# Second FFN's up-projection: the moving operand read from its two halves in turn, with halves and weights at several byte distances

## The chip, the cores and the metric

One core of one Trainium2 chip. The metric is the device time of one execution in microseconds (us), as the median of the runs shown. The engines are TensorE (PE in the profile, with its weight loads as PEld), VectorE (DVE), ScalarE (ACT), GpSimd (POOL) and SyncE (SP), which issues the DMAs.

## The reference, cut to what matters

Two layers over 512 latent tokens and 256 context tokens of 1024 features: layer 0 attention, layer 1 a bidirectional Mamba-2 mixer, each followed by a gated FFN. The change touches the FFN of layer 1, which has the latent tokens alone (512):

```python
def conv_ffn(h, w_up, conv_w, conv_b, w_down):
    g, u = jnp.split(h @ w_up, 2, axis=-1)          # h (512, 1024), w_up (1024, 2 * 2816)
    g = dwconv_centred(g, conv_w, conv_b)           # width 3, along the tokens
    return (jax.nn.silu(g) * u) @ w_down
...
h_l = modulate(rms_norm(x, norm_ffn_w[i]), mod_l[3], mod_l[4])
x = x + mod_l[5] * conv_ffn(h_l, ffn_w_up[i], ffn_conv_w[i], ffn_conv_b[i], ffn_w_down[i])
```

## The kernel before

All activations lie with features on the 128 partitions and tokens along the free dimension, so that 1024 features are KT = 8 tiles of 128x512. Every product is made of three matmuls in fp32r (`mm3`, L100 to L108): a number is split into a high and a low part, and the results of high weight by high activation (L105), high weight by low activation (L106) and low weight by high activation (L108) are summed in PSUM. `split` (L78) makes the parts: ScalarE casts the high part (L85), VectorE subtracts to get the low part (L87). `load_w` (L90) loads a 128x1024 weight tile by DMA on SP's queue into `wst` and splits it into `wh` and `wl`. All three come from one pool tag `t4` with 10 buffers of 4096 bytes.

The second FFN is `ffn(g, 1, ...)`, called at the end of `body`. Its up-projection has 44 weight tiles: f = 0 to 21 for the gate, 22 + f for the other branch. For each f, `up(f)` computes the gate tile (`gemm(f)`, 8 k-steps of three matmuls of 128x512), ScalarE reads it out of PSUM with the middle tap of the convolution (`cv`, L834), VectorE adds the two outer taps, reading the same PSUM tile twice (L838, L839), ScalarE applies SiLU (L840), the second tile `gemm(22 + f)` is computed, VectorE multiplies (`hd`, L849), and the product is split into `hdh` and `hdl`. The hidden tiles of two f are kept; after the first up of the next pair, `down` multiplies them by their two rows of w_down (8 output tiles `ps_d`) and adds the result to x (L785).

PSUM: pool tag S has 2 buffers of two banks each, used for `ps_first` and `ps_up`; pool tag B (`Bank`) has 4 buffers of one bank. The first two up tiles (f = 0 and 22) are not computed in `ffn` but in `first_tiles`, while the norm ahead still produces the modulated activations `h`: in two halves of 256 tokens, with `hhf` (high) written by ScalarE and `hlf` (low) by VectorE or GpSimd. Their two results lie in the two S buffers until `up(0)` has read them. For f = 1 and 23, `gemm` takes a B buffer for that reason (`ps_up1`); all later ones take S.

Within an engine the instructions stand in the order that a scheduler chose from the program's order, the dependences and the buffers; each engine works off its own list in that order and waits on semaphores. SBUF tiles of the second FFN other than weights come from a pool `pg` that is opened after the mixer's pools are closed, with tag `t3` (24 buffers).

Of the kernel before, what the change touches and what calls it, by code (L numbers as in the profile page):

```python
# [7 lines left out]
P = 128  # L8
F32 = mybir.dt.float32
F32R = mybir.dt.float32r  # L10
# [6 lines left out]
KT = D // P  # L17
L = 512
# [49 lines left out]
def t3(g, name, dt=F32, n=T):  # L68
    return g.t3p.tile([P, n], dt, tag="t3", bufs=g.n3, name=name)


def t4(g, name, dt=F32):
    return g.p.tile([P, 1024], dt, tag="t4", bufs=10, name=name)
# [7 lines left out]
def split(g, src, hi, lo, lo_engine="dve", pin=False):  # L81

    nc = g.nc
    keep = g.tc.keep_in_program_order if pin else lambda i: i
    keep(nc.scalar.copy(hi, src))  # L85
    eng = nc.vector if lo_engine == "dve" else nc.gpsimd
    keep(eng.tensor_tensor(lo, src, _r(hi), ALU.subtract))  # L87


def load_w(g, dram, lo_engine="dve", pin=False):  # L90

    st = t4(g, "wst")
    wh = t4(g, "wh", F32R)
    wl = t4(g, "wl", F32R)
    g.nc.sync.dma_start(st, dram)
    split(g, st, wh, wl, lo_engine=lo_engine, pin=pin)
    return wh, wl


def mm3(g, w, outs, first, last):  # L100

    wh, wl = w
    mm = g.nc.tensor.matmul
    for out, (ah, al) in outs:
        mm(out, wh, ah, start=first, stop=False)  # L105
        mm(out, wh, al, start=False, stop=False)  # L106
    for out, (ah, al) in outs:
        mm(out, wl, ah, start=False, stop=last)  # L108
# [106 lines left out]
def follow(g, bi):  # L215

    if g.last_act is not None:
        g.tc.add_manual_dep(bi.ins, g.last_act.ins.name, mybir.DependencyInfo(
            mybir.DependencyClass.NoSync, mybir.DependencyReason.DATA), reason="order of tables")
    g.last_act = bi  # L220


def ln_exp(g):
    follow(g, g.nc.scalar.preload_act_table_set("natural_log_exp_and_others"))
# [77 lines left out]
def S(g, name):  # L302
    return g.ps.tile([P, 1024], F32, tag="S", bufs=2, name=name)


def Bank(g, name):
    return g.ps.tile([P, 512], F32, tag="B", bufs=4, name=name)
# [44 lines left out]
def gemm_in(g, tiles, h, off, segs):  # L352


    for run in segs:
        for ps, w in tiles:
            for k in range(KT):
                ks = slice(k * P, (k + 1) * P)
                mm3(g, (w[0][:, ks], w[1][:, ks]),
                    [(ps[:, off[i] + a : off[i] + b], tuple(t[:, a:b] for t in h[i][k])) for i, a, b in run],  # L360
                    k == 0, k == KT - 1)
                yield


def firsts(g, *units):
    return [load_w(g, u) for u in units]
# [430 lines left out]
def ffn(g, layer, streams, x, h, first, nxt=None, side=iter(()), after=()):  # L797

    nc, I = g.nc, g.I
    ns = len(streams)
    tot = sum(n for n, _ in streams)
    off = [0, L]

    cw = [g.par[:, PC[f"fw{layer}{t}"] : PC[f"fw{layer}{t}"] + NFT] for t in range(3)]
    cb = g.par[:, PC[f"fb{layer}"] : PC[f"fb{layer}"] + NFT]
    whole = [[(i, 0, n) for i, (n, _) in enumerate(streams)]]

    def gemm(t):  # L810

        if t % NFT == 0:
            ps = first[t // NFT]
        else:
            w = load_w(g, I["wup"][layer, t])
            if t % NFT == 1:
                out = []
                for i in range(ns):
                    ps = Bank(g, "ps_up1")
                    for _ in gemm_in(g, [(ps, w)], h, (0, 0), [[s] for s in whole[0] if s[0] == i]):  # L820
                        pass
                    out.append((ps, [i]))
                return [(ps[:, : streams[i][0]], off[i], off[i] + streams[i][0], i) for ps, (i,) in out]
            ps = S(g, "ps_up")
            for _ in gemm_in(g, [(ps, w)], h, off, [[s] for s in whole[0]]):
                pass
        return [(ps[:, :tot], 0, tot, None)]

    def up(f):
        pg = gemm(f)  # L830
        cv = t3(g, "cv", n=tot)
        w0, w1, w2 = (c[:, f : f + 1] for c in cw)
        for ps, a, b, _ in pg:
            nc.scalar.activation(cv[:, a:b], ps, AF.Identity, scale=w1, bias=cb[:, f : f + 1])  # L834
        for i in range(ns):
            a, b = off[i], off[i] + streams[i][0]
            ps, o = next((ps, o) for ps, o, e, j in pg if j in (None, i))
            nc.vector.scalar_tensor_tensor(cv[:, a + 1 : b], ps[:, a - o : b - o - 1], w0, cv[:, a + 1 : b], ALU.mult, ALU.add)  # L838
            nc.vector.scalar_tensor_tensor(cv[:, a : b - 1], ps[:, a - o + 1 : b - o], w2, cv[:, a : b - 1], ALU.mult, ALU.add)  # L839
        follow(g, nc.scalar.activation(cv, cv, AF.Silu))  # L840
        some = (2, 2, 2, 3)[f] if ns > 1 and f < 4 else 1
        for _ in range(some):
            next(side, None)
        pu = gemm(NFT + f)
        for _ in range(some):
            next(side, None)
        hd = t3(g, "hd", n=tot)
        for ps, a, b, _ in pu:
            nc.vector.tensor_tensor(hd[:, a:b], cv[:, a:b], ps, ALU.mult)  # L849
        hi, lo = t3(g, "hdh", F32R, n=tot), t3(g, "hdl", F32R, n=tot)  # L850
        split(g, hd, hi, lo)
        return [(hi[:, off[i] : off[i] + streams[i][0]], lo[:, off[i] : off[i] + streams[i][0]]) for i in range(ns)]

    gate = g.mod[layer][5]
    segs, f = [], 0
    for n in [3] + [2] * 8 + [3] if nxt else [2] * 11:
        segs.append(range(f, f + n))
        f += n
    acts, pend, wf = {}, None, []

    def flush(fs, order, norm=None, after=None):
        ws = [load_w(g, I["wdown"][layer, f * P : (f + 1) * P]) for f in fs]
        if after:
            wf.extend(firsts(g, *after))
        return down(g, ws, [acts.pop(f) for f in fs], gate, streams, x, order, norm, side=side)

    for fs in segs:
        for j, f in enumerate(fs):
            acts[f] = up(f)
            if j == 0 and pend:  # L870
                flush(pend, whole)
        pend = fs
    for _ in side:
        pass
    if nxt:
        ln_exp(g)
    return flush(pend, [[s] for s in ending(streams)], nxt, after), wf
# [378 lines left out]
def body(nc, tc, I, out, dbg=None):  # L1256
    g = Ctx()
# [3 lines left out]
    pool = lambda n, st=es, **k: st.enter_context(tc.tile_pool(name=n, bufs=1, **k))  # L1261
# [31 lines left out]
    x = [[X[:, m, a:b] for m in range(KT)] for a, b in ((0, L), (L, T))]  # L1293
# [23 lines left out]
    phf = ExitStack()  # L1317
# [19 lines left out]

    x, nrm, first = ssd(g, x, nxt, wf, bg, close)
    phf = ExitStack()
    g.t3p, g.n3 = pool("pg", phf), 24  # L1340
    if not (dbg and dbg.get("stage") == 3):
        ffn(g, 1, [(L, 0)], x, nrm.h, first)
    for m in range(KT):
# [103 lines left out]
```

## Time and profile before

| what | value |
|---|---|
| median of the runs (1914.01 and 1917.44) | 1915.72 us |
| span of the profiled execution, first to last instruction | 1908.8 us |
| its time outside the span | not listed; the median is 6.9 us above the span |
| TensorE busy | 1875.1 us (98%) |
| VectorE, ScalarE, GpSimd busy | 1312.3, 820.3, 307.3 us |
| DMA moved | 210.02 MB, 110 GB/s |
| second FFN's up-projection in the span | 1547.7 to 1893 us |

A matmul's row has its start and a duration; since matmuls overlap in the array, the duration (0.39 us for 128x512) is longer than the time that each one adds. The distance from one start to the next is what it adds. In a row of the page's groups, "out<-in" names the tiles, then come partitions x elements, the count, the busy time, the mean duration and the engine's idle time before them. In a table of stretches each engine has its busy time and its number of instructions.

### The profile page before, as it was taken

The page shows a single profiled execution, that of the slowest core. Times are in us where ns is not written, and L with a number is a line of the kernel's source. Part 1 is how long each engine was busy: PE and PEld are TensorE (multiplying, and loading weights), DVE is VectorE, ACT ScalarE, POOL GpSimd, SP SyncE. Part 2 cuts the span into 40 slices and gives each one's busy share as a digit, 9 for nine tenths or more (in the row PEclk, how much of TensorE's full clock was granted, in tenths as well). Part 3 has the DMA queues.
Part 4 walks back from the last instruction along what each step waited for, and adds up shares of the span by engine and source line. Part 5 has one row for each costly group of instructions (what it writes and reads, how often), then busy time and mean ns, then how long its engine had stood idle before and what let it go on. Part 6 is the DMA issues. An engine that isn't in the chain of part 4 may idle for free.

```text
span 1908.8 us, 27505 instructions
## 1 busy us (share of the span) xinstructions
PE 1875.1 (98%) x10834; PEld 1548.3 (81%) x10834; DVE 1312.3 (69%) x1949; ACT 820.3 (43%) x1420; POOL 307.3 (16%) x268
## 2 busy tenths in 40 slices
PE   9999999999999999999999999999999999999999
PEld 7876555688888888888888888888888878888887
DVE  5578778678877777444488777777888466565555
ACT  3534444254122222222266677776667352323331
POOL 2241111031000000000040344444434210000000
PEclk9999998999999999999999999999999999999999
DMA  9221332114434554222123334434443222323232
GB/s 338 78 89 45 114 122 86 34 45 155 154 124 121 186 187 155 67 67 67 59 86 104 110 113 122 122 111 133 121 138 117 89 78 90 99 88 111 88 100 89
DMA packets 73425, 210.02 MB, mean 110 GB/s; under 512 B 8912, under 2 KB 14416, under 8 KB 73168
## 3 DMA queue, kind: packets, MB, share of 16 engines
q1 hardware_dynamic: 73296, 208.26, 34.3%
q8 instruction: 85, 1.39, 0.3%
q14 instruction: 44, 0.36, 0.1%
HBM read 198.79 MB, written 6.82 MB: 108 GB/s over the span
## 4 chain that ended last, share of the span: by engine, by line
PE 76%; DVE 11%; issue 4%; ACT 2%; POOL 2%; DMA 1%; POOLq 0%; DVEq 0%; SPq 0%; ACTq 0%
PE ps_up L108 10%; PE ps_up L106 10%; PE ps_up L105 10%; PE ps_d L105 6%; PE ps_d L106 6%; PE ps_d L108 6%; PE ps_in L106 4%; PE ps_in L108 4%; PE ps_in L105 3%; PE ps_o L638 2%; PE ps_s L674 2%; PE ps_st L1034 1%; DVE Bf L964 1%; PE ps_wo L108 1%; PE ps_wo L105 1%
## 5 line engine op out<-in xcount | busy, mean ns | idle before, releaser
L87 DVE TENSOR_TENSOR wl<-wst,wh 128x1024 fp32r<-128x1024 f32 x205 | 257.3, 1255 | 242.0 <-PE ps_up L106 127.4
L85 ACT CAST wh<-wst 128x1024 fp32r<-128x1024 f32 x211 | 221.2, 1049 | 417.1 <-DMA wst<-in_wup 334.9
L106 PE MATMUL ps_up<-hlf,wh 128*128 128x512 f32 (+1 forms) x1008 | 357.0, 354 | 0.0
L108 PE MATMUL ps_up<-hhf,wl 128*128 128x512 f32 (+1 forms) x1008 | 356.8, 354 | 0.0
L105 PE MATMUL ps_up<-hhf,wh 128*128 128x512 f32 x1008 | 356.8, 354 | 0.0
L106 PEld LDWEIGHTS ps_up<-hlf,wh 128*128 128x128 f32 x1008 | 190.6, 189 | 26.5
L108 PEld LDWEIGHTS ps_up<-hhf,wl 128*128 128x128 f32 x1008 | 190.5, 189 | 26.4
L105 PEld LDWEIGHTS ps_up<-hhf,wh 128*128 128x128 f32 x1008 | 190.5, 189 | 26.4
L105 PE MATMUL ps_in<-hhs,wh 128*128 128x512 f32 (+1 forms) x560 | 204.4, 365 | 1.2 <-ACT dt L919 1.2
L106 PE MATMUL ps_in<-hls,wh 128*128 128x512 f32 (+1 forms) x560 | 199.3, 356 | 0.0
L108 PE MATMUL ps_in<-hhs,wl 128*128 128x512 f32 (+1 forms) x560 | 198.7, 355 | 0.0
L105 PE MATMUL ps_d<-hdh,wh 128*128 128x512 f32 (+1 forms) x568 | 193.9, 343 | 0.2 <-ACT hdh L85 0.2
L108 PE MATMUL ps_d<-hdh,wl 128*128 128x512 f32 (+1 forms) x568 | 193.5, 341 | 0.0
L106 PE MATMUL ps_d<-hdl,wh 128*128 128x512 f32 (+1 forms) x568 | 193.0, 340 | 0.3 <-DVE hdl L87 0.3
L785 DVE SCALAR_TENSOR_TENSOR X<-ps_d,mod,X 128x512 f32<-128x512 f32 (+1 forms) x224 | 124.3, 583 | 35.7 <-PE ps_d L108 35.4
L105 PEld LDWEIGHTS ps_in<-hhs,wh 128*128 128x128 f32 x560 | 105.9, 189 | 16.4 <-ACT dt L919 1.4
L106 PEld LDWEIGHTS ps_d<-hdl,wh 128*128 128x128 f32 x568 | 106.7, 188 | 14.8 <-DVE hdl L87 0.7
L108 PEld LDWEIGHTS ps_in<-hhs,wl 128*128 128x128 f32 x560 | 105.8, 189 | 14.8
L108 PEld LDWEIGHTS ps_d<-hdh,wl 128*128 128x128 f32 x568 | 106.7, 188 | 13.3
L105 PEld LDWEIGHTS ps_d<-hdh,wh 128*128 128x128 f32 x568 | 106.3, 188 | 13.7 <-ACT hdh L85 0.7
L106 PEld LDWEIGHTS ps_in<-hls,wh 128*128 128x128 f32 x560 | 106.0, 189 | 13.2
L677 ACT ACTIVATE pr<-ps_s 128x1024 f32<-128x1024 f32 x56 | 57.2, 1021 | 107.2 <-PE ps_s L676 106.1
(340 smaller groups left out, 3548.6 us busy)
## 6 DMA issues: line engine op xcount, KB each, us to landing
wst<-in_wup SPq DMA_DIRECT2D x88, 512.0 KB, 3.6
wada<-in_adaT SPq DMA_DIRECT2D x56, 512.0 KB, 3.7
wst<-in_win SPq DMA_DIRECT2D x48, 512.0 KB, 3.6
wst<-in_wdown SPq DMA_DIRECT2D x44, 512.0 KB, 4.0
E<-ad SPq DMA_DIRECT2D x64, 256.0 KB, 6.8
wada<-in_adaB SPq DMA_DIRECT2D x24, 512.0 KB, 4.6
ec<-ead SPq DMA_DIRECT2D x64, 128.0 KB, 5.7
wst<-in_wout SPq DMA_DIRECT2D x16, 512.0 KB, 3.6
```

Of the source, the lines that this page charges most:

```text
L85: keep(nc.scalar.copy(hi, src))
L87: keep(eng.tensor_tensor(lo, src, _r(hi), ALU.subtract))
L105: mm(out, wh, ah, start=first, stop=False)
L106: mm(out, wh, al, start=False, stop=False)
L108: mm(out, wl, ah, start=False, stop=last)
L638: nc.tensor.matmul(po[S64[e], :n], v, pr[:, 512 * e + off : 512 * e + off + n], start=first, stop=last)
L674: nc.tensor.matmul(outs[e], a[S64[e], k], b[S64[e], q], start=i == 0, stop=False)
L677: nc.scalar.activation(pr, ps, AF.Exp)
L785: nc.vector.scalar_tensor_tensor(ap, o[:, c0:c1], gate[:, m, v : v + 1], ap, ALU.mult, ALU.add)
L964: i = nc.vector.scalar_tensor_tensor(cv, raw[:, tap : tap + n], par(f"sw{tap}", j), cv, ALU.mult, ALU.add)
L1034: nc.tensor.matmul(ps[:, d * 256 : (d + 1) * 256], Bt[:, t * P : (t + 1) * P], xw[d][t], start=t == ts[0], stop=t == ts[-1])
```

## The change

For layer 1, `ffn` first copies each of the 16 tiles of h (8 high, 8 low) on ScalarE into a new tile `hs`, with the two halves of 256 tokens at a distance of n = 256 + 16 (k mod 4) elements: 1024, 1088, 1152 or 1216 bytes, depending on k. A matmul then reads 16 columns of the first half, 16 of the second, the next 16 of the first, and so on (32 runs of 16 columns), and writes PSUM in the matching order, so that the result lies in PSUM as before. Weight tiles `wh` and `wl` of layer 1 other than the first two come from a new tag `w4` (6 buffers of 1088 elements) and start 8 (t mod 8) elements, that is 0 to 224 bytes in steps of 32, into their buffer. All 42 tiles, f = 1 and 23 too, now take their PSUM tile from S. The pool `pg` has 20 buffers of tag `t3` instead of 24.

```diff
-def load_w(g, dram, lo_engine="dve", pin=False):
+def load_w(g, dram, lo_engine="dve", pin=False, shift=None):
     st = t4(g, "wst")
-    wh = t4(g, "wh", F32R)
-    wl = t4(g, "wl", F32R)
+    if shift is None:
+        wh = t4(g, "wh", F32R)
+        wl = t4(g, "wl", F32R)
+    else:
+        wh, wl = (g.t3p.tile([P, 1024 + 64], F32R, tag="w4", bufs=6, name=n)[:, shift : shift + 1024] for n in ("wh", "wl"))
...
     whole = [[(i, 0, n) for i, (n, _) in enumerate(streams)]]
+    if layer:
+        hs = []
+        for k in range(KT):
+            both = []
+            for src in h[0][k]:
+                n = 256 + 16 * (k % 4)
+                t = g.t3p.tile([P, 640], F32R, tag="hs", bufs=16, name="hs")[:, : 2 * n]
+                t = t.rearrange("p (j x) -> p j x", j=2)[:, :, :256]
+                nc.scalar.copy(t, src.rearrange("p (j x) -> p j x", j=2))
+                both.append(t.rearrange("p j (a e) -> p a j e", e=16))
+            hs.append(tuple(both))
...
         else:
+            if layer:
+                w = load_w(g, I["wup"][layer, t], shift=8 * (t % 8))
+                ps = S(g, "ps_up")
+                out = ps[:, :L].rearrange("p (j a e) -> p a j e", j=2, e=16)
+                for k in range(KT):
+                    ks = slice(k * P, (k + 1) * P)
+                    mm3(g, (w[0][:, ks], w[1][:, ks]), [(out, hs[k])], k == 0, k == KT - 1)
+                return [(ps[:, :tot], 0, tot, None)]
             w = load_w(g, I["wup"][layer, t])
...
-    g.t3p, g.n3 = pool("pg", phf), 24
+    g.t3p, g.n3 = pool("pg", phf), 20
```

Lines below the first edit move on by 3, those behind the second by 22: the three matmuls of `mm3` are L108, L109 and L111 in the changed kernel, and `cv` is L856.

The order of instructions changes where the second FFN begins. ScalarE's list there before, from the last tiles of h (`hhf`, the norm's second half) to the first cv (out of `ps_first`) and the first SiLU:

```order
L290 ACTIVATE hhf_5_14103<-ht,mod_95 128x256
L290 ACTIVATE hhf_6_14105<-ht,mod_95 128x256
L290 ACTIVATE hhf_7_14107<-ht,mod_95 128x256
L834 ACTIVATE cv<-ps_first,par 128x512
L840 ACT_TABLE_LOAD
L840 ACTIVATE cv<-cv 128x512
L85 CAST wh<-wst 128x1024
```

and now, from the last copies (of sixteen that follow each other, all behind the last `hhf`) to the first SiLU:

```order
L820 COPY hs<-hhf_6_14105 128x2x256
L820 COPY hs<-hlf_6_14106 128x2x256
L820 COPY hs<-hhf_7_14107 128x2x256
L820 COPY hs<-hlf_7_14108 128x2x256
L856 ACTIVATE cv<-ps_first,par 128x512
L85 CAST wh<-wst 128x1024 x2
L862 ACT_TABLE_LOAD
L862 ACTIVATE cv<-cv 128x512
```

The sixteen copies stand between the last tile of h and the first cv, and two casts of prefetched weights, which before stood further up among the norm's instructions, now stand behind that cv. TensorE's list at the same place before, where `ps_first_14472` is the second of the first tiles, and `ps_up1` with its number is the result of f = 1 (14643) or 23 (14679) in a bank of its own; this piece stands in the middle of the first tiles:

```order
L105 MATMUL ps_first_14471<-hhf10_0_14093,wh_14294 128x256
L105 MATMUL ps_first_14472<-hhf10_0_14093,wh_14300 128x256
L105 MATMUL ps_up1_14643<-hhf10_0_14093,wh_14638 128x512
L105 MATMUL ps_up1_14679<-hhf10_0_14093,wh_14674 128x512
L106 MATMUL ps_first_14471<-hlf10_0_14094,wh_14294 128x256
L108 MATMUL ps_first_14471<-hhf10_0_14093,wl_14295 128x256
L106 MATMUL ps_first_14472<-hlf10_0_14094,wh_14300 128x256
L108 MATMUL ps_first_14472<-hhf10_0_14093,wl_14301 128x256
L105 MATMUL ps_first_14471<-hhf10_1_14095,wh_14294 128x256
L105 MATMUL ps_first_14472<-hhf10_1_14095,wh_14300 128x256
L106 MATMUL ps_up1_14643<-hlf10_0_14094,wh_14638 128x512
```

and now, with the end of the first tiles and the beginning of f = 1, whose result `ps_up_14675` lies in the first of the two S buffers:

```order
L108 MATMUL ps_first_14472<-hhf10_7_14107,wh_14300 128x256
L109 MATMUL ps_first_14472<-hlf10_7_14108,wh_14300 128x256
L111 MATMUL ps_first_14472<-hhf10_7_14107,wl_14301 128x256
L108 MATMUL ps_up_14675<-hs_14626,wh_14670 128x16x2x16
L109 MATMUL ps_up_14675<-hs_14628,wh_14670 128x16x2x16
L111 MATMUL ps_up_14675<-hs_14626,wl_14671 128x16x2x16
L108 MATMUL ps_up_14675<-hs_14630,wh_14670 128x16x2x16
```

Before, matmuls of f = 1 and 23 were mixed in among those of the first tiles; now all of f = 1 stands behind the last of them, reads `hs`, and its PSUM tile is one that a first tile has to leave.

## The prediction

> **What bounds the kernel now.** I read the page first, then the stretches of the second FFN, then single rows in order of time.
>
> The page: the span, each engine's busy share, the rows of TensorE's busy share and granted clock over 40 slices, and the groups of the up-projection (both layers together).
>
> ```profile
> span 1908.8 us, 27505 instructions
> PE 1875.1 (98%) x10834; PEld 1548.3 (81%) x10834; DVE 1312.3 (69%) x1949; ACT 820.3 (43%) x1420; POOL 307.3 (16%) x268
> ...
> PE   9999999999999999999999999999999999999999
> ...
> PEclk9999998999999999999999999999999999999999
> ...
> L106 PE MATMUL ps_up<-hlf,wh 128*128 128x512 f32 (+1 forms) x1008 | 357.0, 354 | 0.0
> L108 PE MATMUL ps_up<-hhf,wl 128*128 128x512 f32 (+1 forms) x1008 | 356.8, 354 | 0.0
> L105 PE MATMUL ps_up<-hhf,wh 128*128 128x512 f32 x1008 | 356.8, 354 | 0.0
> ```
>
> TensorE is busy in every slice; the granted clock is full but for one slice early on. The second FFN is the last 20% of the span. The table of busy time by stretch (length, then busy us and instructions of TensorE, its weight loads, VectorE, ScalarE and GpSimd, then granted clock, DMA share and GB/s) shows it:
>
> ```profile
> 1580.00:1680.00 100.00, 100.00 (x440) 82.39 (x439) 58.84 (x93) 31.74 (x37) 0.00 (x0) 1.00 0.30 95
> 1680.00:1780.00 100.00, 100.00 (x440) 82.39 (x439) 58.51 (x92) 30.78 (x36) 0.00 (x0) 1.00 0.30 95
> ```
>
> There TensorE has no gap: 440 matmuls in 100 us, 227 ns from one start to the next (down-projections included). VectorE is busy 59%, ScalarE 31%, DMA 30%. So this stage costs what its matmuls cost, and the change touches 42 of 44 up-projection tiles: 42 x 8 x 3 = 1008 matmuls of 128x512. One nanosecond on each is 1.0 us. The durations of rows (390 ns) contain the way through the array; what counts is the distance of starts, so I take first and last rows of runs of matmuls and their count. The settled up-projection:
>
> ```profile
> 1600.04 0.39 PE L105 MATMUL ps_up<-hhf,wh 128*128 128x512 f32 x1
> ...
> 1605.94 0.39 PE L108 MATMUL ps_up<-hhf,wl 128*128 128x512 f32 x1
> ```
>
> 26 distances in 5.90 us: 226.9 ns. What would it be without loss? [...]
>
> ```profile
> L1008 PE MATMUL ps_xt<-cst,xf x96: 271/273/331, 1030.7 to 1418.8; 128*128 128x128 f32 x96
> ...
> L1145 PE MATMUL ps_end<-acsT,cst x4: 326/326/429, 1029.9 to 1030.5; 128*128 128x192 f32 x4
> ...
> L1034 PE MATMUL ps_st<-xw,Bt x160: 377/379/382, 1043.6 to 1440.1; 128*128 128x256 f32 x160
> ...
> 1109.81 2.59 PE ps_st L1034 x12
> ```
>
> 12 in 2.59 us is 215.8 ns for 256 columns, 0.843 ns a column; at the full rate, half of that, 512 columns would take 215.8 ns. The up-projection loses 11 ns of 227 on each. The loss is not fixed by the shape. Rows of the same stage's neighbours, all back to back and without a wait (512 columns with one set of moving tiles, then with another; 256 columns; and the first matmuls of an up-projection after a down-projection):
>
> ```profile
> 1508.87 0.39 PE L106 MATMUL ps_wo<-yl,wh 128*128 128x512 f32 x1
> ...
> 1510.50 0.39 PE L108 MATMUL ps_wo<-yh,wl 128*128 128x512 f32 x1
> ...
> 1511.20 0.39 PE L108 MATMUL ps_wo<-hhy,wl 128*128 128x512 f32 x1
> ...
> 1513.93 0.39 PE L108 MATMUL ps_wo<-hhy,wl 128*128 128x512 f32 x1
> ...
> 1522.50 0.28 PE L105 MATMUL ps_wo<-hhy,wh 128*128 128x256 f32 x1
> ...
> 1524.54 0.28 PE L108 MATMUL ps_wo<-hhy,wl 128*128 128x256 f32 x1
> ...
> 1587.07 0.40 PE L105 MATMUL ps_up<-hhf,wh 128*128 128x512 f32 x1
> ...
> 1589.39 0.39 PE L106 MATMUL ps_up<-hlf,wh 128*128 128x512 f32 x1
> ```
>
> 7 distances in 1.63 us: 232.9 ns; 12 in 2.73: 227.5; 17 in 2.04 with 256 columns: 120.0, where half of 215.8 is 107.9; 10 in 2.32: 232. So the loss is 11 to 17 ns, about as much for 256 columns as for 512, and it depends on which tiles are read and on what ran just before. All these lengths lie near multiples of 6.67 ns (34, 35 and 18 of them), and 6.67 ns is a 64-byte stretch of 16 columns at the full rate. That looks like one or two encounters per matmul between the moving read and the next tile's weight load, which runs beside it at half the pace. I infer this; no row says it.
>
> **The change part by part.**
>
> *Start of the stage: ScalarE's copies and PSUM.* The change adds 16 copies of 128x512 on ScalarE, and tile f = 1 takes a buffer of pool S where it had a bank of its own. S has two buffers and both hold the results of the first two tiles. So TensorE must wait until ScalarE has made the copies, ScalarE has read the first result (behind them in its order), and VectorE has read it twice. The rows of before, ScalarE, VectorE, ScalarE:
>
> ```profile
> 1551.77 0.51 ACT L290 ACTIVATE hhf<-ht,mod 128x256 fp32r<-128x256 f32 x1 [0.32 <-DVE ht L281]
> ...
> 1553.65 0.78 ACT L834 ACTIVATE cv<-ps_first,par 128x512 f32<-128x512 f32 x1 [1.38 <-PE ps_first L108]
> ...
> 1554.63 0.74 DVE L838 SCALAR_TENSOR_TENSOR cv<-ps_first,par,cv 128x511 f32<-128x511 f32 x1
> 1555.40 0.75 DVE L839 SCALAR_TENSOR_TENSOR cv<-ps_first,par,cv 128x511 f32<-128x511 f32 x1
> ...
> 1566.18 0.62 ACT L85 CAST hdh<-hd 128x512 fp32r<-128x512 f32 x1 [2.93 <-DVE hd L849]
> 1566.71 1.04 ACT L85 CAST wh<-wst 128x1024 fp32r<-128x1024 f32 x1
> ```
>
> The last h is issued at 1551.77 and a form like it gives up the engine after about 0.4 us: the copies begin at 1552.2. A cast of 128x512 between SBUF tiles takes 1566.71 - 1566.18 = 0.53 us until the next: 16 x 0.53 = 8.5, to 1560.7. From the start of the first cv (1553.65) to the end of VectorE's second read (1555.40 + 0.75) were 2.5 us: to 1563.2. Only then does TensorE begin f = 1.
>
> ```profile
> 1554.72 0.28 PE L106 MATMUL ps_first<-hlf,wh 128*128 128x256 f32 x1
> ...
> 1565.19 0.39 PE L105 MATMUL ps_up<-hhf,wh 128*128 128x512 f32 x1
> ```
>
> Before, the last of the first tiles was issued at 1554.72, and the two tiles of f = 1 (some of their matmuls already slipped in between the first tiles) were through at 1565.19, where f = 2 begins. After: 1563.2 + 48 x 0.2269 = 1574.1. That is 8.9 us later. The wait leaves TensorE idle for about 8 us. When it had waited for some us in the norm just ahead, the clock was then granted at half (0.50) for 3.4 us:
>
> ```profile
> 1538.40:1541.80 3.40, 3.38 (x16) 3.38 (x17) 3.40 (x9) 2.24 (x5) 0.84 (x1) 0.50 0.00 0
> ```
>
> I add half of that, 1.7 us. Off goes something: two ScalarE casts and two VectorE subtractions of prefetched weights that stood in the norm now come after it,
>
> ```profile
> 1535.49 1.04 ACT L85 CAST wh<-wst 128x1024 fp32r<-128x1024 f32 x1
> ...
> 1536.56 1.23 DVE L87 TENSOR_TENSOR wl<-wst,wh 128x1024 fp32r<-128x1024 f32 x1
> ```
>
> about 0.95 us of ScalarE and 1.2 us of VectorE in the way of the norm's second half; I take off 1.1 us. Sum: 8.9 + 1.7 - 1.1 = 9.5 us. The bounds: 7 (no clock loss, both subtractions gained) and 12 (twice the clock loss, no gain, slower strided copies).
>
> *Buffers.* Weight tiles of the second FFN get six buffers of their own (three tiles), the shared pool of ten is left to the loads: one tile more is prefetched, cost nothing, since TensorE does not wait now. Twenty t3 buffers for 24: two pairs of hidden tiles and the working ones are about 12; nothing waits. Past the start, ScalarE and VectorE have the instructions they had, at 31% and 59% busy; if that cover went, TensorE would show gaps again.
>
> *The matmuls.* Each of the 1008 now reads and writes 32 runs of 16 columns. Two unknowns. First, what a change of run costs. The nearest rows are the ones above: ps_end reads its 192 columns as six runs of 32 with gaps, median 326 ns, exactly between 273 for 128 and 379 for 256 contiguous columns (326). Nothing per run, at half the rate; its writes are contiguous. I take nothing; the upper bound is that the walk misses one column at half the rate, 0.84 ns, at every run: 27 ns a matmul. Second, what becomes of the loss. With halves read in turn the moving read advances through each half at half the pace, like the weight load, and like the half-rate rows, which lose nothing. If the two collide only when they run at different paces, they now collide at first or not at all, and a collision pushes the moving read out of step. Lower bound: 215.8 ns, 11.1 us off 1008 matmuls. Upper bound: 240, two steps of 6.67 above now: 13.4 us on. The 32 combinations of distance and weight position average over good and bad ones; I take one step of 6.67 off, 220.2 ns: -6.7 us.
>
> Sum against the profiled execution: 1908.8 + 9.5 - 6.7 = 1911.6 us of span. Its time outside the span is not listed; the median of the runs (1915.72) is 6.9 above the span, so 1918.5.
>
> [...]
>
> **The rivals.**
>
> *The pitch stays at 227.* The loss would then have nothing to do with where the streams run. For it: 512 columns lose the same 11 ns through all of the last 300 us. Against: 227.5 and 232.9 for equal shapes with other tiles. Time: 1908.8 + 9.5 + 6.9 = 1925.2. [...]
>
> *More collisions.* Both halves of a step lie in the same place of a 256-byte period for a quarter of the k, and the position changes every three matmuls, so the streams never settle; the unsettled rows cost 232, two steps more 240. Time: 5 to 13.4 us more: 1930 to 1939.
>
> *Every run costs (the other side).* Place: the step from one half to the other in the moving read, 32 times a matmul. One half-rate column each is 27 us (1952), two are 54.4 us: 1979.6. It decides (2%, 38.3 us, less 9.5 of the start) from 28.6 ns a matmul, 0.89 ns a run. For it: at the full rate there is half the time to find the next address that ps_end had. Against: ps_end's 326.
>
> *Writes in runs halve the rate.* 512 columns at 0.843 are 432 ns: 205 us more, 2130. Nothing in the rows speaks for it or against.
>
> **How the numbers follow.** Forecast (214 to 224 ns): 0.38; its own range is 1911 to 1925. Pitch stays: 0.24. More collisions: 0.18. Every run costs: 0.15. Half the rate: 0.05. Predicted is the likeliest, 1918. The range leaves out the last two, 0.20: from 1910 (no loss, smallest start) to 1945. Faster by over 2% (1877) is outside every bound here: 0.01. Slower by over 2% (1954, about what a measurement can tell from no change): half the rate, and 0.11 of the case in which runs cost: 0.16. Within 2%: 0.83.
>
> **What would show it.** Right: sixteen hs copies of about 0.53 us ahead of the first cv; TensorE idle for 7 to 9 us before the first ps_up, with a stretch of half clock behind it; f = 2 beginning 8 to 11 us later than now; no gaps after that; starts of ps_up 214 to 224 ns apart, differing with k (distance of halves) and with the tile (weight position). Wrong: starts at 227 throughout; starts far above 240, equal for all k and tiles, which would be a price of runs or of writes; gaps between tiles, which would be the buffers; ps_up of f = 1 beginning beside the first tiles.

## The result: 1.2% slower

| | before | after |
|---|---|---|
| median of the runs (2 each) | 1915.72 us (1914.01 to 1917.44) | 1932.88 us (1930.38 to 1935.38) |
| ratio after to before, 95% interval | | 1.0116 [1.0085, 1.0147] |
| span of the profiled execution | 1908.8 us | 1928.6 us |
| mean granted clock | 0.995 | 0.993 |

The ratio means +16 to +28 us; the two medians differ by 17.2 (0.9%) and the two spans by 19.8. The changed kernel ended inside the forecast range, above the forecast by 14 us. The start of the stage came out about as predicted; the matmuls went the other way.

The page after: span, TensorE's busy time and instructions, granted clock over 40 slices, and one of the three groups of turned matmuls (busy us, mean ns of one, idle time ahead and what ended it).

```profile
span 1928.6 us, 27522 instructions
PE 1889.5 (98%) x10834; PEld 1551.0 (80%) x10834; DVE 1309.0 (68%) x1949; ACT 827.6 (43%) x1436; POOL 307.1 (16%) x268
PEclk9999999999999999999999999999999989999999
L108 PE MATMUL ps_up<-hs,wh 128*128 128x512 f32 x336 | 137.2, 408 | 8.0 <-ACT wh L85 8.0
```

TensorE has the same 10834 instructions. The 1008 turned ones stand in groups of their own, by line; this one holds the only wait, 8.0 us, and one slice now has a lower clock: that is the start of the stage. The page's share of 98% hides what else has happened, because a slower matmul is still a busy TensorE. It shows in the count of matmuls in the same two stretches as before (440 in each there):

```profile
1580.00:1680.00 100.00, 100.00 (x424) 79.72 (x423) 55.77 (x89) 28.52 (x35) 0.00 (x0) 1.00 0.27 92
1680.00:1780.00 100.00, 100.00 (x423) 79.75 (x422) 57.03 (x90) 30.09 (x36) 0.00 (x0) 1.00 0.27 93
```

No gap, full clock, and 16 or 17 matmuls fewer in 100 us. First and last row of a settled tile, 20 distances apart:

```profile
1600.78 0.40 PE L109 MATMUL ps_up<-hs,wh 128*128 128x512 f32 x1
1605.60 0.41 PE L108 MATMUL ps_up<-hs,wh 128*128 128x512 f32 x1
```

4.82 us: 241.0 ns from start to start, where it was 226.9. Over all 1008 the median is 241.0 and more than half of them lie between 240 and 242. It hardly depends on the places: 240.7, 240.6, 242.4 and 241.2 for the four distances of the halves, 239.7 to 244.5 for the 32 pairs of distance and weight shift.

The start of the stage in the rows of TensorE, ScalarE, VectorE and the weight loads (PEld), and the clock behind it:

```profile
1548.87 0.28 PE L111 MATMUL ps_first<-hhf,wl 128*128 128x256 f32 x1
1557.16 0.77 PE L108 MATMUL ps_up<-hs,wh 128*128 128x512 f32 x1 [8.01 <-ACT wh L85]
...
1546.24 0.62 ACT L820 CAST hs<-hhf 128x512 fp32r<-128x512 f32 x1 [0.73 <-DVE hlf L294]
1554.04 0.61 ACT L820 CAST hs<-hlf 128x512 fp32r<-128x512 f32 x1
1554.56 0.77 ACT L856 ACTIVATE cv<-ps_first,par 128x512 f32<-128x512 f32 x1
1555.23 1.98 ACT L85 CAST wh<-wst 128x1024 fp32r<-128x1024 f32 x2
...
1555.42 0.75 DVE L860 SCALAR_TENSOR_TENSOR cv<-ps_first,par,cv 128x511 f32<-128x511 f32 x1 [6.44 <-ACT cv L856]
1556.20 0.75 DVE L861 SCALAR_TENSOR_TENSOR cv<-ps_first,par,cv 128x511 f32<-128x511 f32 x1
...
1558.14 0.29 PEld L111 LDWEIGHTS ps_up<-hs,wl 128*128 128x128 f32 x1 [0.51 <-DVE wl L87]
...
1557.10:1562.60 5.50, 5.44 (x13) 4.00 (x14) 5.25 (x6) 4.42 (x6) 0.00 (x0) 0.50 0.60 177
```

Sixteen casts of 0.52 us each, then one ScalarE read and two VectorE reads of the first result, and only then, at 1557.16, the first up-projection of f = 1. The row's releaser names the weight cast on L85 behind the first cv. The first of those two casts ends at about 1556.2; the end of the second VectorE read, 1556.20 + 0.75, is the one that lies against 1557.16. The weights of f = 1 are late too, though: they are cast only behind the copies and the first cv, and the third matmul's weight load waits 0.51 us for their low part. With these lists of instructions a PSUM bank of its own for f = 1 would have saved less than 1 us of the wait. Then 5.5 us at half clock; the granted clock had fallen at 1552.8, still within the wait.

Where the 19.8 us of span come from, comparing the start of the same matmul in both traces: 4.2 us earlier in the last matmuls ahead of the norm (the part that the change does not touch ran that much faster in this execution); 6.3 us later when f = 2 begins, so the start costs 10.5; 19.8 us later at the last matmul, so the other 960 matmuls of the stage cost 13.5 us, spread evenly.

### The profile page after: what moved, and what is told of

Read it like the earlier page. It is cut to its first block, busy times and chain, and to the rows that moved or that the text cites. A ratio compares the mean times of both kernels' runs of the same rounds, so it can differ in the third digit from the quotient of the medians.

```text
span 1928.6 us, 27522 instructions
## 1 busy us (share of the span) xinstructions
PE 1889.5 (98%) x10834; PEld 1551.0 (80%) x10834; DVE 1309.0 (68%) x1949; ACT 827.6 (43%) x1436; POOL 307.1 (16%) x268
## 4 chain that ended last, share of the span: by engine, by line
PE 81%; DVE 9%; issue 3%; ACT 2%; POOL 1%; DMA 0%; DVEq 0%; POOLq 0%; ACTq 0%
PE ps_up L108 10%; PE ps_up L109 10%; PE ps_up L111 10%; PE ps_d L108 6%; PE ps_d L109 6%; PE ps_d L111 6%; PE ps_in L111 4%; PE ps_in L109 4%; PE ps_in L108 4%; PE ps_o L641 2%; PE ps_s L677 2%; PE ps_st L1056 2%; DVE ht L284 1%; PE ps_wo L111 1%; PE ps_wo L108 1%
## 5 line engine op out<-in xcount | busy, mean ns | idle before, releaser
L85 ACT CAST wh<-wst 128x1024 fp32r<-128x1024 f32 x211 | 221.2, 1049 | 495.8 <-DMA wst<-in_wup 207.4
L109 PE MATMUL ps_up<-hlf,wh 128*128 128x256 f32 (+1 forms) x672 | 226.3, 337 | 0.0
L108 PE MATMUL ps_up<-hhf,wh 128*128 128x512 f32 (+1 forms) x672 | 225.9, 336 | 0.0
L111 PE MATMUL ps_up<-hhf,wl 128*128 128x256 f32 (+1 forms) x672 | 225.9, 336 | 0.0
L108 PE MATMUL ps_in<-hhs,wh 128*128 128x512 f32 (+1 forms) x560 | 204.4, 365 | 1.2 <-ACT dt L941 1.2
L109 PE MATMUL ps_in<-hls,wh 128*128 128x512 f32 (+1 forms) x560 | 199.4, 356 | 0.0
L111 PE MATMUL ps_in<-hhs,wl 128*128 128x512 f32 (+1 forms) x560 | 198.7, 355 | 0.0
L109 PE MATMUL ps_d<-hdl,wh 128*128 128x512 f32 (+1 forms) x568 | 193.8, 342 | 0.2 <-DVE hdl L87 0.2
L108 PE MATMUL ps_d<-hdh,wh 128*128 128x512 f32 (+1 forms) x568 | 193.2, 342 | 0.3 <-ACT hdh L85 0.2
L111 PE MATMUL ps_d<-hdh,wl 128*128 128x512 f32 (+1 forms) x568 | 192.9, 340 | 0.0
L108 PE MATMUL ps_up<-hs,wh 128*128 128x512 f32 x336 | 137.2, 408 | 8.0 <-ACT wh L85 8.0
L108 PEld LDWEIGHTS ps_up<-hhf,wh 128*128 128x128 f32 x672 | 127.5, 190 | 13.5
L109 PEld LDWEIGHTS ps_up<-hlf,wh 128*128 128x128 f32 x672 | 127.5, 190 | 13.1
L111 PEld LDWEIGHTS ps_up<-hhf,wl 128*128 128x128 f32 x672 | 127.4, 190 | 13.0
L111 PE MATMUL ps_up<-hs,wl 128*128 128x512 f32 x336 | 136.9, 407 | 0.0
L109 PE MATMUL ps_up<-hs,wh 128*128 128x512 f32 x336 | 136.8, 407 | 0.0
L108 PEld LDWEIGHTS ps_in<-hhs,wh 128*128 128x128 f32 x560 | 105.9, 189 | 16.4 <-ACT dt L941 1.4
L109 PEld LDWEIGHTS ps_d<-hdl,wh 128*128 128x128 f32 x568 | 106.8, 188 | 14.3 <-DVE hdl L87 0.6
L108 PEld LDWEIGHTS ps_d<-hdh,wh 128*128 128x128 f32 x568 | 106.3, 188 | 14.7 <-ACT hdh L85 0.7
L111 PEld LDWEIGHTS ps_in<-hhs,wl 128*128 128x128 f32 x560 | 105.8, 189 | 14.7
```

## The experiments

Every kernel here is the changed kernel with the edit shown, but for one that starts from the kernel before. Pitch means the distance from start to start of two matmuls in ns, as a mean or median over the rows of a kind at full clock (the two differ by less than 2 ns); the first three of a tile, which follow another kind of work, are left out. "Before" is the kernel before on the same chip. A time without a ratio is that of a single execution; such kernels are judged by their pitches.

**Which part of a turned matmul is slow: length of the run, reading or writing, start of the run.** In these three the copies are plain tiles with halves 1024 bytes apart and the weights stand unshifted.

```diff
+                e = (16, 8, 32, 64, 128, 256)[t % 6]
+                turn = lambda v: v.rearrange("p (j a e) -> p a j e", j=2, e=e) if e < 256 else v
+                out = turn(ps[:, :L])
...
+                    mm3(g, (w[0][:, ks], w[1][:, ks]), [(out, tuple(turn(v) for v in hs[k]))], k == 0, k == KT - 1)
```

> The changed kernel with the halves always 1024 bytes apart, weights at one place, and the length of a run set by the tile: 16, 8, 32, 64, 128 columns or none (contiguous), in turn. If each run costs one column's time on top of the old loss (0.42 ns x number of runs + 226.9 ns): 240 with 32 runs (16 columns), 253.6 with 64 runs, 233.6 with 16, 230.2 with 8, 228.6 with 4, 227 contiguous. If each run costs two columns and the old loss is gone (215.8 + 0.83 x runs): 242, 269, 229, 222, 219. If the weight loads collide with a read at the wrong pace: no order by number of runs; 8 columns would be about as 16 (both advance at half the pace), contiguous 227.

1919.38 us in one run (before 1904.73). Pitch with runs of 8, 16, 32, 64, 128 columns and contiguous: 243.4, 240.0, 236.9, 226.7, 227.2, 226.7. First and last rows of a tile with 16, with 64 and with 32 columns, in this order, 20 distances each:

```profile
1574.38 0.40 PE L108 MATMUL ps_up<-hs,wh 128*128 128x512 f32 x1
1579.18 0.40 PE L111 MATMUL ps_up<-hs,wl 128*128 128x512 f32 x1
...
1591.09 0.39 PE L108 MATMUL ps_up<-hs,wh 128*128 128x512 f32 x1
1595.62 0.39 PE L111 MATMUL ps_up<-hs,wl 128*128 128x512 f32 x1
...
1607.84 0.40 PE L108 MATMUL ps_up<-hs,wh 128*128 128x512 f32 x1
1612.58 0.40 PE L111 MATMUL ps_up<-hs,wl 128*128 128x512 f32 x1
```

4.80, 4.53 and 4.74 us. So there is a price on short runs and none at 64 columns, but it is no price per run: twice the runs (8 columns) adds 3.4 ns to the 13.3 of 16 columns, half of them (32) takes off 3.1.

The first tile of this kernel (f = 1, runs of 8) begins at half clock, as f = 1 does behind the wait of 8.0 us in the changed kernel and in that with the start alone. Nine distances of it at half clock, then nine at full clock; below them nine at half clock of the same tile in the kernel that reads contiguously without shifts (the start alone, further down):

```profile
1555.41 0.63 PE L108 MATMUL ps_up<-hs,wh 128*128 128x512 f32 x1
1559.25 0.63 PE L108 MATMUL ps_up<-hs,wh 128*128 128x512 f32 x1
...
1560.34 0.41 PE L108 MATMUL ps_up<-hs,wh 128*128 128x512 f32 x1
1562.53 0.40 PE L108 MATMUL ps_up<-hs,wh 128*128 128x512 f32 x1
```

```profile
1555.03 0.63 PE L108 MATMUL ps_up<-hs,wh 128*128 128x512 f32 x1
1558.87 0.63 PE L108 MATMUL ps_up<-hs,wh 128*128 128x512 f32 x1
```

3.84, 2.19 and 3.84 us: 426.7, 243.3 and 426.7 ns. At half clock the shortest runs cost exactly what contiguous reads cost, twice 213.3: both the price of the runs and the 11 ns of the contiguous read are there at full clock only. So the price is no fixed number of TensorE cycles and no fixed time per run; what it is at full clock these rows do not say.

```diff
+                turn = lambda v: v.rearrange("p (j a e) -> p a j e", j=2, e=16)
+                rd, wr = ((turn, turn), (turn, lambda v: v), (lambda v: v, turn))[t % 3]
+                out = wr(ps[:, :L])
...
+                    mm3(g, (w[0][:, ks], w[1][:, ks]), [(out, tuple(rd(v) for v in hs[k]))], k == 0, k == KT - 1)
```

In two of three tiles the columns of the result are permuted here, since only the read or only the write is turned.

> Three kinds of tiles in turn: runs of 16 columns both read and written (as in the change), read in runs but written contiguously, read contiguously but written in runs. In the last two kinds the columns of the result come out in another order, so the output is not the reference's. If the price lies in the moving read (or in its collisions with weight loads): about 241, 241 and 227 ns from start to start. If it lies in the writes to PSUM: 241, 227, 241. If it takes both: 241, 227, 227.

1922.03 us (before 1904.73). Both turned 240.0, only the read 240.0, only the write 227.2. The rows of a tile with the read turned, then of one with the write turned:

```profile
1596.74 0.40 PE L111 MATMUL ps_up<-hs,wl 128*128 128x512 f32 x1
1601.54 0.40 PE L109 MATMUL ps_up<-hs,wh 128*128 128x512 f32 x1
...
1624.71 0.39 PE L111 MATMUL ps_up<-hs,wl 128*128 128x512 f32 x1
1629.24 0.39 PE L109 MATMUL ps_up<-hs,wh 128*128 128x512 f32 x1
```

4.80 and 4.53 us for 20: the whole price is on the moving operand's read. Writing PSUM in runs of 16 costs nothing: 226.5 ns in the rows that only write so.

```diff
+                o = 4 * (k % 4)
+                t = g.t3p.tile([P, 640], F32R, tag="hs", bufs=16, name="hs")[:, o : o + 512]
+                nc.scalar.copy(t, src)
+                both.append(t.rearrange("p (j a e) -> p a j e", j=2, e=16))
```

> The changed kernel with the halves always 1024 bytes apart, weights at one place, and the copies of h starting 0, 16, 32 or 48 bytes further on with k mod 4. If a run of 64 bytes costs because it begins in the middle of a 64-byte piece of memory and so touches two: 240 ns for three of the four starts and about 227 or less for the one that is aligned (32 bytes on). If a run costs in itself: 240 to 241 for all four. If collisions with the weight load decide: the four differ by 6 ns and more, in no such order.

1928.72 us (before 1904.73). Starts moved by 0, 16, 32, 48 bytes: 239.4, 240.2, 240.1, 242.6. Only one of the four starts can lie on a 64-byte boundary, and none is near 227: the alignment of the runs moves the pitch by 3 ns at most and is not the cause.

**What the shifts of the weights do, and what the start costs.** Contiguous reads in both; the first keeps the eight weight shifts of the changed kernel, the second has none.

```diff
-                out = ps[:, :L].rearrange("p (j a e) -> p a j e", j=2, e=16)
+                out = ps[:, :L]
```

> The changed kernel with all of it (copies of h, PSUM buffers, weights at eight places, buffer counts) but the turns: the matmuls read the copies contiguously. If the turns cost what the profile of the change shows (14 ns x 1008 = 14 us) and the start of the stage the rest (9.7 us): 9 to 10 us over the kernel before, ratio 1.005, and 227 ns from start to start. If places of weights and activations matter for contiguous reads (collisions): 216 to 234 ns, by tile, different for the eight weight places. If the whole loss is at the start: 20 us over.

1919.55 us, ratio 1.0078 [1.0061, 1.0095], +12 to +18 us. Pitch with the weights 0, 32, 64, 96, 128, 160, 192 and 224 bytes further, modulo 256, than the moving tile: 227.4, 233.0, 233.2, 234.0, 232.5, 233.1, 229.0, 233.4. A tile at 0 and one at 32 bytes:

```profile
1576.67 0.39 PE L109 MATMUL ps_up<-hs,wh 128*128 128x512 f32 x1
1581.22 0.39 PE L108 MATMUL ps_up<-hs,wh 128*128 128x512 f32 x1
...
1598.74 0.40 PE L109 MATMUL ps_up<-hs,wh 128*128 128x512 f32 x1
1603.40 0.40 PE L108 MATMUL ps_up<-hs,wh 128*128 128x512 f32 x1
```

4.55 and 4.66 us for 20, 227.5 and 233.0. The expected 227 throughout did not come; the pitch goes by tile, as the reading by places had it. So with contiguous reads the place of the weights against the moving tile is worth up to 7 ns a matmul, and 0, the place that the buffer sizes of the kernel before give, is the best of the eight. The places here and below are worked out from the kernels' buffer sizes; no trace lists an address. The mean is 231.9: about 5 us over 1008, which with the start (9.7 by the same comparison) is the 14.8 us measured. Shifts and turns do not add: the shifts alone cost 5 ns, the turns alone 13.3, both together 14.

```diff
-                w = load_w(g, I["wup"][layer, t], shift=8 * (t % 8))
+                w = load_w(g, I["wup"][layer, t], shift=0)
...
-                out = ps[:, :L].rearrange("p (j a e) -> p a j e", j=2, e=16)
+                out = ps[:, :L]
```

> The changed kernel without the turns and without the shifts: the sixteen copies and the new order of the first tiles stay, the copies are read contiguously, the weights stand at the same place modulo 256 bytes as the copies. My reading: matmuls at 227 ns as before, and the start alone costs 9 to 10 us: ratio 1.0045 to 1.0055. Rival (the buffers that were taken from the pool, 24 to 20, and the lost half of the B banks also cost something further on): +12 us or more.

1912.88 us, ratio 1.0045 [1.0027, 1.0062]: +5 to +12 us. The first up-projection matmul behind the copies waits as in the changed kernel, and later stretches hold 442 matmuls in 100 us:

```profile
1553.46 0.77 PE L108 MATMUL ps_up<-hs,wh 128*128 128x512 f32 x1 [7.96 <-ACT wh L85]
...
1600.00:1700.00 100.00, 100.00 (x442) 82.55 (x441) 58.63 (x92) 31.93 (x38) 0.00 (x0) 1.00 0.28 95
```

Against the trace of before the same matmul is 7.9 us earlier ahead of the norm and 2.2 later behind the start: 10.1 us. Afterwards nothing is lost. The smaller pool of hidden tiles and the lost banks cost nothing here.

```diff
-            if layer:
+            if layer and t % NFT > 1:
                 w = load_w(g, I["wup"][layer, t], shift=8 * (t % 8))
```

> The first two tiles of the stage are computed as before, straight from the norm's tiles and without waiting for the copies; the other 960 matmuls are turned as in the changed kernel. My reading of the changed kernel (start +9.7 us, 1008 matmuls at +14 ns): the start's part goes, what stays is 960 x 14 ns = +13.4 us, ratio to the kernel before 1.006 to 1.008, and the first matmul of the stage starts within 1 us of where it did. Rival (the copies and conversions delay the norm and the engines beside it however late they are used): ratio stays near 1.011.

1919.09 us, ratio 1.0069 [1.0048, 1.0091]: +9 to +17 us. Compared with before, the same matmul is 4.9 us earlier ahead of the norm, 4.6 earlier when f = 2 begins, 8.9 later at the end: the start's cost is gone (0.3 left), and 960 matmuls cost 13.5 us, 14.1 ns each, with a pitch of 241.0. The parts add up: 10 us for the start by itself, 13.5 for the matmuls by themselves.

**Is it a collision with the weight load?** The prediction explained the loss of a matmul as meetings of the moving read with the next tile's weight load. A load of fewer weight columns is shorter, so less should be lost. The kernel uses only 128, 64 or 32 columns of the weights in a tile (the first and last matmul of a tile keep 128), so part of the product is left out.

```diff
+                c = (128, 64, 32)[t % 3]
+                turn = (lambda v: v.rearrange("p (j a e) -> p a j e", j=2, e=16)) if t // 3 % 2 else (lambda v: v)
...
+                    mm(turn(ps[:c, :L]), wh[:, :c], al, start=False, stop=False)
```

> The weights of the product are cut to 128, 64 or 32 of their columns (tile by tile), so part of the product is left out; the moving operand stays 512 columns, read contiguously or in turns of 16, weights at the same place modulo 256 bytes. Theory 1: a 512-column matmul needs about 215.8 ns by itself and the rest of the pitch (11 ns contiguous, 24 ns turned) is the load of the next weights getting in the way; the rest then scales with the weight columns: contiguous 226.7, about 221, about 218.5; turned 240, about 228, about 222. Theory 2: the turned read is slower in itself: turned minus contiguous stays 13 ns at 128, 64 and 32 weight columns, whatever the contiguous pitch does.

1920.09 us (before 1905.36). The loads themselves take 188, 135 and 111 ns in this trace: 0.83 ns a column from 64 to 128 and 0.75 from 32 to 64, about half the pace of a contiguous moving read (226.7 ns by 512 columns is 0.44), as the prediction had it. Turned: 240.0, 240.0, 240.0 with 128, 64, 32 weight columns. Contiguous: 227.0, 230.0, 232.0. A tile with 32 weight columns read contiguously (18 distances), then one read in turn (21):

```profile
1607.35 0.40 PE L838 MATMUL ps_up<-hs,wh 128*32 128x512 f32 x1
1611.52 0.40 PE L838 MATMUL ps_up<-hs,wh 128*32 128x512 f32 x1
...
1623.45 0.40 PE L839 MATMUL ps_up<-hs,wh 128*32 128x512 f32 x1
1628.49 0.40 PE L839 MATMUL ps_up<-hs,wh 128*32 128x512 f32 x1
```

4.17 us by 18 is 231.7; 5.04 by 21 is 240.0. A quarter of the weights does not shorten a matmul by anything: the turned pitch stays, the contiguous one grows by 5 ns. The length of the load is not what is lost. The first theory falls. The second (a price of the turned read in itself) fits the turned rows, but not the difference that it named: 13 ns falls to 8, because the contiguous rows grow.

**Is it the length of the run, or the going to and fro?** First one kernel with a layout for each k, then two with settled tiles.

```diff
+        LAY = [(first_(flat), flat), (gap(32, 16, 20), runs(16)), (first_(turn(2, 16)), turn(2, 16)), (gap(8, 64, 80), runs(64)),
+               (first_(turn(4, 16)), turn(4, 16)), (gap(2, 256, 304), runs(256)), (gap(16, 32, 40), runs(32)), (first_(turn(2, 32)), turn(2, 32))]
...
```

> Each of the eight k of a tile reads its copy in another layout (weights at shift 0, the product unchanged, the accumulator written in the matching order). Known from the runs before: contiguous 227, halves in turn with runs of 16 240, of 32 237. Theory 1 (the price is on the length of a run, wherever the next run lies): runs of 16 that follow one another with a gap of 4 columns also 240, runs of 32 with a gap of 8 also 237, runs of 64 with a gap of 16 columns 227, four quarters in turn with runs of 16 also 240. Theory 2 (the price is on going to and fro between two far places): runs with gaps 227 whatever their length; four quarters in turn 240 or more. Two runs of 256 with a gap: 227 by both.

1929.54 us (before 1908.71). With layouts that change every three matmuls the pitch depends on the neighbours too: contiguous, which is 227 among its like, is 231.8 here. Means: runs of 16 with a gap 239.5, two halves with 16 240.6, runs of 64 with a gap 233.8, four quarters with 16 233.5, two runs of 256 228.5, runs of 32 with a gap 231.7, two halves with 32 236.7. The gap of 16 speaks for the first theory, the four quarters for neither; for the rest this run is inconclusive.

```diff
+                j, e = ((2, 16), (4, 16), (8, 16), (16, 16), (4, 32), (8, 32))[t % 6]
+                turn = lambda v: v.rearrange("p (j a e) -> p a j e", j=j, e=e)
...
```

> Tile by tile the same contiguous copies (weights at shift 0) are read in turn from 2, 4, 8 or 16 places, 16 columns each (places 1024, 512, 256 and 128 bytes apart), and from 4 or 8 places with 32 columns each. Theory 1 (the price is on the length of the run): 240 for all four with runs of 16, 237 for both with runs of 32. Theory 2 (it is on the distance between the places): 240 at 1024 bytes, where the mixed run before suggests about 229 at 512 bytes and then 227 or another value at 256 and 128 bytes; runs of 32 follow the distance likewise.

1922.26 us (before 1905.48). Runs of 16 from 2, 4, 8, 16 places: 240.0, 232.0, 239.5, 240.0. Runs of 32 from 4 and 8 places: 233.0 and 236.0. Neither theory gives the 232 and 233 of four places. A tile with four places, 20 distances in 4.64 us:

```profile
1596.53 0.41 PE L111 MATMUL ps_up<-hs,wl 128*128 128x512 f32 x1
1601.17 0.40 PE L109 MATMUL ps_up<-hs,wh 128*128 128x512 f32 x1
```

```diff
+                t = g.t3p.tile([P, 640], F32R, tag="hs", bufs=16, name="hs")
+                t = t.rearrange("p (a w) -> p a w", w=20)[:, :, :16]
+                nc.scalar.copy(t, src.rearrange("p (a e) -> p a e", e=16))
...
```

> All tiles read runs of 16 columns that follow one another with a gap of 4 columns (80 bytes from run to run), weights at shift 0: never back to an earlier place. Theory 1 (length of the run): 240 ns. Theory 2 (to and fro between two places 1024 bytes apart): 227 ns. The mixed run before gave 239.5 between neighbours of other layouts, which speaks for the first.

1930.91 us (before 1905.48). 243.0, with no way back at all (the three tiles after the first stand at 237.9, all later ones at 243.3; why is open):

```profile
1599.17 0.40 PE L111 MATMUL ps_up<-hs,wl 128*128 128x512 f32 x1
1604.04 0.40 PE L109 MATMUL ps_up<-hs,wh 128*128 128x512 f32 x1
```

4.87 us for 20. The second theory falls: forward steps of 80 bytes cost as much as jumps of 1024. The first holds for runs of 16, but for four places 512 bytes apart, where 232 stands against 240. Why that one is cheaper stays open.

**A version that uses what the runs showed.** By before's own rows and its buffer sizes 256-column matmuls stand at 119.6 ns where weights and moving tile have the same place modulo 256 bytes, and at 115.1 where the weights are 64 bytes further. This kernel is the kernel before with only those places moved.

```diff
-    g.h = [[htiles(g, n, f"a{i}_{m}") for m in range(KT)] for i, n in enumerate((L, C))]
+    hc = [htiles(g, C, f"a1_{m}") for m in range(KT)]
+    nc.vector.memset(g.p.tile([P, 16], F32, name="pad"), 0.0)
+    g.h = [[htiles(g, L, f"a0_{m}") for m in range(KT)], hc]
```

> The kernel before, with one thing moved: the 256-column moving tiles stand 64 bytes below their weights modulo 256 instead of at the same place (a pad of 16 columns between the two groups of tiles, whose order is swapped). By the kernel before's own trace a 256-column matmul takes 119.6 ns at distance 0 and 115.1 ns at 64; some 1800 matmuls move from the one to the other. If the place modulo 256 bytes is the cause: -8 us, up to -11 us by the medians (120 and 114 ns), ratio 0.994 to 0.996. If the difference between those rows belongs to the stages and not to the place: ratio 0.999 to 1.001 and the 256-column matmuls of the first FFN stay at 120 ns.

1902.97 us (before 1905.36, 12 and 19 runs), ratio 0.9982 [0.9971, 0.9994]: 1 to 6 us faster. First and last of the 24 matmuls with 256 columns of one tile of the first FFN, in the kernel before and then here:

```profile
600.03 0.28 PE L105 MATMUL ps_up<-hhf,wh 128*128 128x256 f32 x1
602.78 0.28 PE L108 MATMUL ps_up<-hhf,wl 128*128 128x256 f32 x1
```

```profile
595.42 0.28 PE L105 MATMUL ps_up<-hhf,wh 128*128 128x256 f32 x1
598.13 0.28 PE L108 MATMUL ps_up<-hhf,wl 128*128 128x256 f32 x1
```

23 distances in 2.75 and 2.71 us: 119.6 and 117.8. In the other projections of 256 columns (ps_in) the median falls from 120 to 114, as expected, in these rows only to 117 or 118; rows of ps_c, which read tiles of the same group with other weights, rise from 114 to 119. So the place acts, but the gain (2.4 us by the medians) is a third of the 8 us that I had expected, and the ratio lies between the two ranges that I had named. This version beats both kernels.

## Why the prediction was right or wrong

*Start of the stage: right, 9.5 us predicted, 10.5 measured* (10.1 in the trace of the start by itself, where the runs give 5 to 12). The copies were 0.52 us each for 0.53, the reads of the first result 2.4 us for 2.5, the wait 8.0 for "about 8". Three sizes were off and partly cancelled: the half clock lasted 5.5 us, not the 3.4 of the shorter wait that I took as its row, which is 2.8 us lost for 1.7; the norm gained about 2 us, where I took off 1.1; and the first copy waited 0.73 us for the last low tile, which the sum has at nothing.

*Buffers: right.* No wait after the start, in the changed kernel or with the start alone.

*The cost of a change of run: the row did not carry over.* I took "nothing" from ps_end, which reads runs of 32 at about half the rate (0.843 ns a column in the rows beside it, 0.443 in the contiguous up-projection). For half the pace that was right: at half clock even runs of 8 cost nothing (426.7 ns, as contiguous). At the full rate runs of 32 cost 6 to 10 ns a matmul and runs of 16 mostly 13 (four places 5, forward with a gap 16). I had written against it myself, in the rival, that at the full rate there is half the time to find the next address, and then given that rival 0.15.

*The loss: the failed step is "I take one step of 6.67 off, 220.2 ns: -6.7 us".* In its place stand 241 ns and +14 us: the term had the wrong sign and is 20 us off, partly offset in the spans by a common part that was 4.2 us faster. The step rested on the inference that the 11 ns of a contiguous matmul are collisions that turns would break up. The runs took it apart. Narrower weights do not lower the pitch (240.0 turned, 227 to 232 contiguous), the halves' distance and the weights' shift move the turned pitch by 2 to 5 ns only, and the read alone brings the whole 13 ns. The 215.8 ns without loss were my estimate, from plain fp32 rows taken to run at half the rate; no run shows them for 512 columns at full clock, where the lowest settled pitches are 226.5 to 227. Half the rate is about what the trace of before shows: 256 columns take 215.9 ns in the plain fp32 rows (ps_st) at full clock, and 213.3 in fp32r at half clock (1538.4 to 1541.8). What the 11 ns are is still open, and so is why a short run costs; the traces show only that both are gone at half clock.

*The rival "more collisions"* had the right size, 240 ns and 1930 to 1939, and the runs fell into it, but not for its reason: a meeting with the weight load should depend on the places and on the load's length, and the turned rows stand between 239.7 and 244.5 for all 32 pairs and at 240.0 with a quarter of the load. *"Every run costs"* had the right place, the moving read, and a wrong law: 0.84 ns a run would have been 27 ns, with 54 at 8 columns; 13.3 and 16.7 were measured. *Writes in runs* cost nothing (227.2). *"The pitch stays at 227"* is what runs of 64 columns do (226.7).

The time lies in the upper part of the range, which was drawn wide enough for the pitch that stays and for more collisions; the forecast's own range ended at 1925. That the time fell inside is luck as far as the mechanism goes: a price of short runs was in the range's account only as a case left out, and it came out at half the 27 ns that I had given it. Of the sign that I named for being wrong (starts far above 240, equal for all k and tiles) the trace shows the second half, at 241.

## What to carry to other kernels

Read the moving operand of a 512-column fp32r matmul contiguously, or in runs of at least 64 columns (tried here with two halves in turn, 226.7 ns); runs of 32 or less cost 5 to 17 ns of 227 at full clock here, while turning the written side was free (227.2). Where a stage has no gaps, count matmuls per 100 us or the distance of starts: the busy share cannot show that each of them has become slower (440 in 100 us before and 424 after, TensorE 100% busy both times). Before a stage is changed so that all its inputs are copied first, look at what the copies push behind them on their engine (here the first cv, 0.77 us, and two casts of weights, 1.98 us), and add the half clock that follows the wait (5.5 us of TensorE's work here, behind 8.0 us).

## What the runs showed of the hardware that was not expected

- The pitch of contiguous fp32r matmuls goes with the distance of weights and moving tile modulo 256 bytes, as far as buffer sizes give it: 227.4 at 0, 229.0 at 192, 232.5 to 234.0 elsewhere for 512 columns (weights moved); 120 at 0 and 114 to 118 at 64 for 256 columns (moving tiles moved), the other way round. It is not the distance alone, since 114 and 118 stand at the same one. Multiples of 256 bytes show no difference: with the start alone, where buffers of 4352 bytes (weights) and 2560 (moving tiles) give many of them, 442 matmuls in 100 us are 226.2 ns each on average.
- At half clock a 512-column matmul takes 426.7 ns whether it reads contiguously or in runs of 8; at full clock these are 226.7 and 243.4.
- Several settled pitches stand on a ladder: 226.7, 233.2 and 240.0 are 34, 35 and 36 times 6.67 ns to 0.3 ns, and 236.9 and 243.4 lie near half steps. Others do not (229.0, 232).
- A weight tile of 32 columns makes a contiguous 512-column matmul slower, not faster: 232 against 227 ns.
- Around the wait of 8.0 us the granted clock was half for 10.2 us (1552.8 to 1563.0), TensorE working in a little over 5.5 of them; in the norm ahead, in the kernel before, after waits of 0.3 to 1.0 us, it was half for 3.4 (1538.4 to 1541.8).
